# A hybrid attention layer on one core: the first pair's weight sums through small tiles, and the order in which the pairs of gate tiles begin

## The chip, the cores and the metric

The kernel runs on one core of one Trainium2 chip. The metric is device time in microseconds for one execution; lower is better. The time given for a version is the median of its runs.

## The reference

One decoder layer over 2048 tokens of width 1024 (plus 16 meta tokens in front). The rows of x are normed, multiplied by one wide matrix `w_in`, and the 6400 columns of the product go to two attentions and to gates:

```
xn = rms_norm(h, norm_gain)
proj = xn @ w_in                       # 1024 x 6400
sb_q, sb_k, sb_v, sw_q, sw_k, sw_v, sb_z, sw_z, g_sb, g_sw = split(proj)
o_sb = stick_breaking_attention(sb_q, sb_k, sb_v)
o_sw = sliding_window_sink_attention(rope(sw_q), rope(sw_k), sw_v, sinks)
y_sb = (o_sb * silu(sb_z)) @ w_branch_sb
y_sw = (o_sw * silu(sw_z)) @ w_branch_swa
merged = sigmoid(g_sb) * y_sb + sigmoid(g_sw) * y_sw
out = rms_norm(h + merged @ w_out, final_norm_gain)
```

The change concerns the columns `sb_z`, `sw_z`, `g_sb` and `g_sw`, the "gates": 28 column tiles of 128 columns each.

## The kernel before

**Numbers in two parts.** Every float32 operand of a matmul is split into a high part (a cast copy, on ScalarE) and a low part (the operand less the high part, on VectorE), and a product is three matmuls: high by high, high by low, low by high. A column tile of `w_in` is 128 x 1024; as weights it is 8 blocks of 128 x 128, high and low.

**The order of the work.** The tokens are worked in two halves of two groups of 512 (`halves`, line 1145). In each half come the projections with the sliding-window attention, then the stick-breaking attention, woven with gate tiles so that TensorE is fed, then the remaining gate tiles as "pairs". The branch and output projections (`finish`) stand at the end. TensorE's order is written out by hand (`manual_schedule`). The orders of ScalarE, VectorE and SyncE, which issues all DMAs, come from a planner: it runs through the program in an estimate of time, takes what is ready, earlier program text first, and gives tiles their buffers as these come free. Each engine's queue then runs strictly in that order.

**Gate tiles.** `gate` (line 580 on) asks for the tile's weights, multiplies them with the two groups (`gemm`, lines 415 to 417: 24 matmuls of 512 columns a group), takes a sigmoid on ScalarE (line 583) and stores the result. `weights` (line 167) loads a raw tile (512 KB), splits it (lines 109 and 112), and stores both parts to DRAM so that the second half can load them instead (`kept`). The weight buffers are a ring `wh`/`wl` of three tiles, the raw buffers a ring `raw` of two. `tmp` (line 344) is a ring of seven tiles of 128 x 512 that nearly all the helpers share.

**Pairs.** From gate tile 14 (counted from 0) on in half 0 (`REST[0] + 2`) and 20 in half 1, two column tiles are computed together by seven products of half-depth blocks in place of eight (the method of Strassen and Winograd). A pair's operands are sums of quarters. On the side of x they are made once a half by `sums_of_x` (lines 589 to 629): t1 to t4, some 50 VectorE instructions, in two steps. On the side of the weights `pair_weights` (line 631) makes t1 (the tile a as it is: quarters "11" and "12"), t3 (sums "s2" and "s3"), t2 ("s1" and "22", a plain quarter), and t4 ("s4"). t1, t3 and t2 each take one of the three `wh`/`wl` buffers. Pairs whose plain quarters half 1 wants as ordinary tiles (`plain`) also store those; the others store the sums for half 1 (`kept[key]`, in DRAM as p0 to p3).

`seven` (line 682) is a pair's matmuls in three parts: 11 (with 12, if `lead`), the middle (s2, 12 if not `lead`, s1, s3, 22), then s4. A product is 12 matmuls (line 688). The sum with product 11 at line 703 must be done before s3 may go on in the same PSUM bank. `in_line` (line 739) sets the order: the first pair's weights, the second step of the sums of x, pair one's 11 and 12, its middle, pair two's weights and 11, pair one's s4, and so on. Only the first pair of a half is `lead`.

**The early weights.** The first pair's weight sums of half 0 are made much earlier, at the start of the stick-breaking stage, between the second and third gate tile (lines 1354 to 1358): `pair_weights(..., early=True)` fills all three `wh`/`wl` buffers and five `tmp` tiles, stores the sums and the plain quarters (14 stores), and lets the buffers go. When the pairs begin, the sums are loaded again. The third gate tile's `weights` follows it in the program.

Of the kernel before, what the change touches and what calls it, by code (L numbers as in the profile page):

```python
# [17 lines left out]
P = 128  # L18
# [29 lines left out]
def tile_kernel(ctx, tc, x, xt, meta, metat, gain, w_in, w_sb, w_sw, w_out, sinks, fgain,  # L48
# [579 lines left out]
            parted("t4", k, b21)  # L628
        yield q

    def pair_weights(bp, ca, cb, plain, early=False):

        t1, t3, t2 = ([wp.tile([P, KT, P], F32R, tag=t, name=t, bufs=3) for t in ("wh", "wl")] for _ in range(3))
        if early:
            t4 = [tmp(F32R).rearrange("p (k c) -> p k c", k=KT // 2) for _ in range(2)]
        else:
            t4 = [bp.tile([P, KT // 2, P], F32R, tag=t, name=t, bufs=2) for t in ("s4h", "s4l")]
        key = w_in.name, ca, cb
        if key in kept:
            for ts, ks in zip((t1, t3, t2, t4), kept[key]):  # L640
                for t, k in zip(ts, ks):
                    DMA(t, k)
        else:
            a, b = load(ca), load(cb)
            s = tp.tile([P, KT, P], F32, tag="vt", name="s", bufs=1)
            s4 = tmp().rearrange("p (k c) -> p k c", k=KT // 2)
            lo, hi = slice(0, KT // 2), slice(KT // 2, KT)

            def parts(hl, t):
                A.copy(hl[0], t)  # L650
                V.tensor_tensor(hl[1], t, f32(hl[0]), op=ALU.subtract)
            parts(t1, a)
            if plain:
                t5 = [tmp(F32R).rearrange("p (k c) -> p k c", k=KT // 2) for _ in range(2)]
                parts(t5, b[:, lo])
            V.tensor_tensor(s[:, hi], a[:, lo], b[:, lo], op=ALU.subtract)
            V.tensor_tensor(b[:, lo], b[:, lo], b[:, hi], op=ALU.add)
            V.tensor_tensor(s[:, lo], b[:, lo], a[:, lo], op=ALU.subtract)
            parts(t3, s)
            parts(t2, b)  # L660
            V.tensor_tensor(s4, a[:, hi], s[:, lo], op=ALU.subtract)
            parts(t4, s4)
            if plain:
                for c in (ca, cb):
                    kept[w_in.name, c] = [dram(f"{e}_{w_in.name}_{c}", [P, KT, P], F32R) for e in "hl"]
                for k, t in zip(kept[w_in.name, ca], t1):
                    DMA(k, t)
                for k, t, u in zip(kept[w_in.name, cb], t5, t2):
                    DMA(k[:, lo], t)
                    DMA(k[:, hi], u[:, hi])  # L670
            if early or not plain:
                kept[key] = []
                for n, ts in enumerate((t1, t3, t2, t4)):
                    kept[key].append([dram(f"p{n}{e}_{ca}", list(t.shape), F32R) for e, t in zip("hl", ts)])
                    for k, t in zip(kept[key][n], ts):
                        DMA(k, t)
        (t1h, t1l), (t3h, t3l), (t2h, t2l) = t1, t3, t2
        lo, hi = slice(0, KT // 2), slice(KT // 2, KT)
        return {"11": (t1h[:, lo], t1l[:, lo]), "12": (t1h[:, hi], t1l[:, hi]), "s2": (t3h[:, lo], t3l[:, lo]),
                "s3": (t3h[:, hi], t3l[:, hi]), "s1": (t2h[:, lo], t2l[:, lo]), "22": (t2h[:, hi], t2l[:, hi]), "s4": t4}  # L680

    def seven(w, b, tag, use, lead):

# [37 lines left out]
    def gate_pair(bp, ga, gb, groups, q, tag, plain, lead, times):  # L721
        tiles = ga, gb

        def use(m, n, t):
            c0, dst, silu, src = tiles[m]
            e = tmp()
            A.activation(e, t, AF.Sigmoid)
            if silu:
                V.tensor_tensor(e, t, e, op=ALU.mult)
            if times:  # L730
                o = ring_x()
                DMA(o, src[groups[n]])
                V.tensor_tensor(e, e, o, op=ALU.mult)
            DMA(dst[groups[n]], e)
        w = pair_weights(bp, ga[0], gb[0], plain)
        yield
        yield from seven(w, q, tag, use, lead)

    def in_line(pairs):

        for n, g in enumerate(pairs):
            if n == 0:
                next(g)
                yield n
                next(g)
            next(g)
            if n + 1 < len(pairs):
                next(pairs[n + 1])
                next(pairs[n + 1])
            drain(g)  # L750
            yield n

# [553 lines left out]
    for half, groups in enumerate(halves):  # L1306
# [42 lines left out]
        with tc.tile_pool(name=f"sb{half}", bufs=1, side="left") as bp:  # L1349
            hsplit[0] = vsplit[0] = True  # L1350
            next_sums = {g: sums() for g in halves[1]} if half == 0 else {}
            side = stick(groups, bp, [(x[g * GT + i * P:g * GT + (i + 1) * P, f * GT:(f + 1) * GT], ssq[:, f, i:i + 1])
                                      for g, ssq in next_sums.items() for i in range(4) for f in range(2)])
            drain(tiles_by_tile(gts[1:2], groups))
            rest = REST[half]
            if half == 0:
                pair_weights(None, gss[0][rest + 2][0], gss[0][rest + 3][0], True, True)
            drain(tiles_by_tile(gts[2:3], groups))
            cost_sb = 8 * sum(4 * (4 - g) for g in groups) * 1.31 + 8 * 0.75
            ratio = cost_sb / ((rest - 3) * 10.4)  # L1360
            weave(tiles_by_tile(gts[3:rest], groups), side, ratio)
            drain(side)
        with tc.tile_pool(name=f"pairs{half}", bufs=1, side="left") as bp:
            ts = [mk() for mk in gts[rest:rest + 2]]
            sums_q = sums_of_x(bp, groups)
            tq = next(sums_q)
            for n, (w, use, _) in enumerate(ts):
                for i, g in enumerate(groups):
                    drain(lagged(col_tile(w, g, use, bank="gz"[i])))
            order = gss[half]  # L1370
            todo = in_line([gate_pair(bp, order[n], order[n + 1], groups, tq, ("o", "zm")[n // 2 % 2],
                                      half == 0 and n < PLAIN, n == rest + 2, half == 0) for n in range(rest + 2, 26, 2)])
            next(todo)
            next(sums_q)
            for n in todo:
                if half == 0 and n == 4:
                    t, u = (tmp()[:, :8] for _ in range(2))
                    for n, ssq in enumerate(next_sums.values()):
                        V.tensor_tensor(t[:, 4 * n:4 * n + 4], ssq[:, 0], ssq[:, 1], op=ALU.add)
                    rs = tp.tile([P, 8], F32, tag="rs8", name="rs", bufs=1)  # L1380
                    rsqrt(rs, t, tp, t=u)
                    rs0, rs1 = rs[:, :4], rs[:, 4:]
# [71 lines left out]
```

## Time and profile before

| | |
|---|---|
| median of 3 runs | 2140.8 us (2137.91 to 2143.49) |
| the profiled execution | 2139.68 us |
| its span, first to last instruction | 2138.0 us |
| mean granted TensorE clock | 0.995 |
| DMA queue of the kernel | 395.26 MB, 54.5% of 16 engines' span |

The profile shows one execution. PE is TensorE's matmuls, PEld its weight loads, DVE VectorE, ACT ScalarE, POOL GpSimd, SP SyncE; "SPq" is a DMA's time in SyncE's queue. A line of a view in order of time gives the start, the duration, the engine, the source line, the operation, the tile written and the tiles read, and in brackets the idle time before it and what ended it. "L109" is line 109 of the kernel. In the view of stages the columns are the length, then each engine's busy time, the granted clock, the DMA share and GB/s.

The 40 slices of the page, of 53.5 us each, show where TensorE is not full: the first slice and the last, and the eighth and thirteenth with an 8, the former with the clock at 9 tenths.

```profile
PE   8999999899998999999999999999999999999998
PEclk9999999899999999999999999999999999999999
```

### The profile page before, as it was taken

To read this page: it belongs to the slowest core of one execution; us is meant where nothing else is said; L and a number is where in the kernel's file an instruction comes from. 1 tells how busy PE (TensorE), PEld (TensorE's weight loads), DVE (VectorE), ACT (ScalarE), POOL (GpSimd) and SP (SyncE) were. 2 spreads that over 40 slices of the span, in tenths; PEclk is the share of its full clock that TensorE was granted. 3 is DMA by queue.
4 is the path that set the end of the run, shared out by engine and by line. 5 is a ranking of instruction groups with operands and counts; after the bars stand their busy time and mean duration, and the time that the engine had idled before them with its cause. 6 is when DMAs were issued, how large, how long until landed. Compare 5 with 4: busy or idle time off the path is not lost.

```text
span 2138.0 us, 29936 instructions
## 1 busy us (share of the span) xinstructions
PE 2091.8 (98%) x10426; PEld 1736.9 (81%) x10426; DVE 1497.1 (70%) x2389; ACT 1079.3 (50%) x2442; POOL 184.1 (9%) x373
## 2 busy tenths in 40 slices
PE   8999999899998999999999999999999999999998
PEld 7788887678877888888888888888888888887887
DVE  7897885578887863777756888989996336554453
ACT  6677774566643343677754656656552312221121
POOL 2122331000000000122210000000000000000000
PEclk9999999899999999999999999999999999999999
DMA  9855544975446985444446333333226786558532
GB/s 340 301 169 191 180 166 171 348 226 176 151 147 214 339 306 177 152 147 146 154 159 186 116 107 119 124 119 108 81 89 217 263 322 197 191 204 284 156 111 79
DMA packets 181142, 397.16 MB, mean 186 GB/s; under 512 B 23456, under 2 KB 41696, under 8 KB 180992
## 3 DMA queue, kind: packets, MB, share of 16 engines
q1 hardware_dynamic: 180992, 395.26, 54.5%
q8 instruction: 82, 1.34, 0.3%
q14 instruction: 68, 0.56, 0.1%
HBM read 245.74 MB, written 149.37 MB: 185 GB/s over the span
## 4 chain that ended last, share of the span: by engine, by line
PE 82%; DVE 8%; DMA 5%; ACT 3%; issue 2%; SPq 1%; DVEq 0%; ACTq 0%
PE ps_g L415 11%; PE ps_g L417 11%; PE ps_g L416 11%; PE ps_o L1106 5%; PE ps_t L1075 5%; PE ps_z L1050 5%; PE ps_o L934 3%; PE ps_z L888 2%; PE ps_z L688 2%; PE ps_t L688 2%; PE ps_g L688 2%; PE ps_g L237 1%; PE ps_g L238 1%; PE ps_g L236 1%; PE ps_z L238 1%
## 5 line engine op out<-in xcount | busy, mean ns | idle before, releaser
L415 PE MATMUL ps_g<-xh,wh 128*128 128x512 f32 x1224 | 503.2, 411 | 19.1 <-ACT wh L109 12.3
L416 PE MATMUL ps_g<-xl,wh 128*128 128x512 f32 x1224 | 481.4, 393 | 0.0
L417 PE MATMUL ps_g<-xh,wl 128*128 128x512 f32 x1224 | 481.2, 393 | 0.0
L415 PEld LDWEIGHTS ps_g<-xh,wh 128*128 128x128 f32 x1224 | 231.8, 189 | 56.1 <-ACT wh L109 12.7
L417 PEld LDWEIGHTS ps_g<-xh,wl 128*128 128x128 f32 x1224 | 230.7, 188 | 52.6 <-DVE wl L112 0.8
L416 PEld LDWEIGHTS ps_g<-xl,wh 128*128 128x128 f32 x1224 | 232.2, 190 | 36.0 <-DVE xl L1159 1.3
L1053 ACT ACTIVATE row<-ps_z 128x512 f32<-128x512 f32 (+2 forms) x320 | 165.4, 518 | 180.0 <-PE ps_z L1050 176.5
L1062 DVE TENSOR_TENSOR_SCAN row<-row 128x528 f32<-128x528 f32 (+1 forms) x192 | 210.6, 1097 | 19.8 <-ACT row L1053 15.4
L116 DVE SCALAR_TENSOR_TENSOR wtl<-ps_t,wth 128x512 fp32r<-128x512 f32 (+1 forms) x320 | 189.7, 593 | 18.5 <-ACT wth L115 17.8
L115 ACT ACTIVATE wth<-ps_t 128x512 fp32r<-128x512 f32 (+1 forms) x320 | 170.6, 533 | 58.3 <-PE ps_t L1075 56.0
L1060 DVE TENSOR_TENSOR_SCAN row<-row,mask 128x512 f32<-128x512 f32 (+4 forms) x128 | 144.2, 1131 | 69.1 <-ACT row L1053 68.0
L1050 PE MATMUL ps_z<-kt,q 128*128 128x512 f32 (+4 forms) x640 | 178.9, 355 | 0.0
L1075 PE MATMUL ps_t<-ident,row 128*128 128x128 f32 x1088 | 171.9, 273 | 6.3 <-DVE wtl L116 3.8
L1075 PEld LDWEIGHTS ps_t<-ident,row 128*128 128x128 f32 x1088 | 134.4, 140 | 41.1 <-DVE wtl L116 6.7
L1050 PEld LDWEIGHTS ps_z<-kt,q 128*128 128x128 f32 x640 | 117.4, 188 | 22.1 <-ACT row L1053 0.4
L1106 PE MATMUL ps_o<-wth,vc 128*128 128x512 f32 (+1 forms) x320 | 130.7, 409 | 1.0 <-ACT tmp L1110 0.9
L896 ACT ACTIVATE sc<-sc,nm 128x129 f32<-128x129 f32 x256 | 100.0, 393 | 40.9 <-DVE nm L894 40.2
L1106 PE MATMUL ps_o<-wtl,vc 128*128 128x512 f32 (+1 forms) x320 | 117.1, 366 | 0.2
L112 DVE TENSOR_TENSOR wl<-raw,wh 128x1024 fp32r<-128x1024 f32 (+1 forms) x51 | 58.4, 1145 | 45.6 <-ACT wh L109 40.8
L1066 POOL COPY xs<-row 128x16 f32<-128x16 f32 x128 | 28.8, 225 | 668.8 <-DVE row L1062 590.1
L583 ACT ACTIVATE tmp<-ps_g 128x512 f32<-128x512 f32 x72 | 43.1, 598 | 65.2 <-PE ps_g L417 60.2
L301 ACT ACTIVATE sq<-res 128x512 bf16<-128x512 f32 x32 | 20.2, 632 | 109.3 <-DVE res L297 107.0
(421 smaller groups left out, 4132.5 us busy)
## 6 DMA issues: line engine op xcount, KB each, us to landing
wh<-h_in_w_in SPq DMA_DIRECT2D x60, 512.0 KB
wl<-l_in_w_in SPq DMA_DIRECT2D x60, 512.0 KB
raw<-in_w_in SPq DMA_DIRECT2D x50, 512.0 KB
h_in_w_in<-wh SPq DMA_DIRECT2D x41, 512.0 KB
l_in_w_in<-wl SPq DMA_DIRECT2D x41, 512.0 KB
q<-qd SPq DMA_DIRECT2D x128, 128.0 KB
vc<-vd SPq DMA_DIRECT2D x48, 256.0 KB
kd<-tmp SPq DMA_DIRECT2D x32, 256.0 KB
```

The costliest lines, as they stand in the source:

```text
L115: A.activation(h, acc, AF.Copy, scale=scale)
L116: V.scalar_tensor_tensor(l, acc, scale, f32(h), op0=ALU.mult, op1=ALU.subtract)
L415: T.matmul(acc, lhsT=wh[:, k, :], rhs=xh[g][:, k, :], start=k == 0, stop=False)
L416: T.matmul(acc, lhsT=wh[:, k, :], rhs=xl[g][:, k, :], start=False, stop=False)
L417: T.matmul(acc, lhsT=wl[:, k, :], rhs=xh[g][:, k, :], start=False, stop=k == KT - 1)
L688: T.matmul(acc, lhsT=l[:, k, :], rhs=r[:, k, :], start=first and k == i == 0, stop=k == KT // 2 - 1 and i == 2, skip_group_check=not (firs ...
L1050: T.matmul(acc[:, :b - a], lhsT=lq, rhs=kt[h][:, k0 + a:k0 + b], start=t == 0, stop=t == 1)
L1053: A.activation(r[:, a:b], acc[:, :b - a], AF.Sigmoid, scale=-1.0)
L1060: V.tensor_tensor_scan(r[:, :w], r[:, :w], mask[0][:, :w], 1.0, op0=ALU.mult, op1=ALU.max)
L1062: V.tensor_tensor_scan(r[:, :w], r[:, :w], r[:, :w], last[j], op0=ALU.mult, op1=ALU.min)
L1075: T.transpose(tr[:, j * P:(j + 1) * P], rows_of[h, g, n - (j > i), j][:, k0:k0 + P], ident)
L1106: T.matmul(o[:, :n], lhsT=v, rhs=r, start=first and r is wh, stop=last and r is wl)
```

## The change

Three things are edited.

1. `pair_weights(..., early=True)` becomes a function of its own, `early_weights`. It makes the same sums, but a quarter (128 x 512) at a time, each in two `tmp` tiles, and stores each quarter to where it belongs, a plain one that is also a kept tile's to both places: 22 stores of 256 KB. It takes no `wh`/`wl` buffer. It works in place on the raw tiles: the last sum is taken from the first tile's raw buffer.
2. At the start of the stick-breaking stage the second and third gate tiles' weights are both asked for before the early weights, and their matmuls come after it. TensorE's order there stays as it was.
3. `pair_weights` gives t1 first and the rest later; the first two pairs of each half are `lead` instead of the first; and `in_line` begins with 11 and 12 of pair one, 11 and 12 of pair two, and then pair one's middle. Of a later pair t1 and product 11 still stand ahead of the s4 of the pair before, and the rest of its weights is asked for after that.

```diff
+    def early_weights(ca, cb):
+        key = w_in.name, ca, cb
+        kept[key] = [[dram(f"p{n}{e}_{ca}", [P, 4 if n == 3 else KT, P], F32R) for e in "hl"] for n in range(4)]
+        for c in (ca, cb):
+            kept[w_in.name, c] = [dram(f"{e}_{w_in.name}_{c}", [P, KT, P], F32R) for e in "hl"]
+        plain_a, plain_b = (kept[w_in.name, c] for c in (ca, cb))
+        t1, t3, t2, t4 = kept[key]
+        a, b = load(ca), load(cb)
+        lo, hi = slice(0, KT // 2), slice(KT // 2, KT)
+        def part(t, *dst):
+            for e in range(2):
+                u = tmp(F32R).rearrange("p (k c) -> p k c", k=KT // 2)
+                if e == 0:
+                    h = u
+                    A.copy(u, t)
+                else:
+                    V.tensor_tensor(u, t, f32(h), op=ALU.subtract)
+                for d, cs in dst:
+                    DMA(d[e][:, cs], u)
+        s = tp.tile([P, KT, P], F32, tag="vt", name="s", bufs=1)
+        part(a[:, lo], (t1, lo), (plain_a, lo))
+        part(a[:, hi], (t1, hi), (plain_a, hi))
+        part(b[:, lo], (plain_b, lo))
+        part(b[:, hi], (t2, hi), (plain_b, hi))
+        V.tensor_tensor(s[:, hi], a[:, lo], b[:, lo], op=ALU.subtract)
+        part(s[:, hi], (t3, hi))
+        V.tensor_tensor(b[:, lo], b[:, lo], b[:, hi], op=ALU.add)
+        part(b[:, lo], (t2, lo))
+        V.tensor_tensor(s[:, lo], b[:, lo], a[:, lo], op=ALU.subtract)
+        part(s[:, lo], (t3, lo))
+        V.tensor_tensor(a[:, hi], a[:, hi], s[:, lo], op=ALU.subtract)
+        part(a[:, hi], (t4, lo))
...
+    def pair_weights(bp, ca, cb, plain):
...
+        t1 = ring("11", "12")
+        key = w_in.name, ca, cb
+        old = kept.get(key)
+        if old:
+            fill(t1, old[0])
         else:
             a, b = load(ca), load(cb)
+            A.copy(t1[0], a)
+            V.tensor_tensor(t1[1], a, f32(t1[0]), op=ALU.subtract)
+        yield w
+        t3, t2 = ring("s2", "s3"), ring("s1", "22")
+        t4 = w["s4"] = [bp.tile([P, KT // 2, P], F32R, tag=t, name=t, bufs=2) for t in ("s4h", "s4l")]
+        if old:
+            for ts, ks in zip((t3, t2, t4), old[1:]):
+                fill(ts, ks)
...
-        w = pair_weights(bp, ga[0], gb[0], plain)
+        ws = pair_weights(bp, ga[0], gb[0], plain)
+        w = next(ws)
         yield
-        yield from seven(w, q, tag, use, lead)
+        products = seven(w, q, tag, use, lead)
+        next(products)
+        yield
+        next(ws)
+        yield
+        yield from products
 
     def in_line(pairs):
 
+        first, second = pairs[:2]
+        next(first)
+        yield 0
+        for step in (first, first, second, second):
+            next(step)
         for n, g in enumerate(pairs):
-            if n == 0:
-                next(g)
-                yield n
+            if n:
                 next(g)
             next(g)
-            if n + 1 < len(pairs):
-                next(pairs[n + 1])
-                next(pairs[n + 1])
+            for more in pairs[n + 1:n + 2] if n else ():
+                next(more)
+                next(more)
             drain(g)
             yield n
...
-            drain(tiles_by_tile(gts[1:2], groups))
             rest = REST[half]
+            ts = [mk() for mk in gts[1:3]]
             if half == 0:
-                pair_weights(None, gss[0][rest + 2][0], gss[0][rest + 3][0], True, True)
-            drain(tiles_by_tile(gts[2:3], groups))
+                early_weights(gss[0][rest + 2][0], gss[0][rest + 3][0])
+            for t in ts:
+                drain(by_group([t], groups))
...
-                                      half == 0 and n < PLAIN, n == rest + 2, half == 0) for n in range(rest + 2, 26, 2)])
+                                      half == 0 and n < PLAIN, n < rest + 6, half == 0) for n in range(rest + 2, 26, 2)])
```

More of the change, by code (lines that the diff above doesn't have):

```diff
@@ L629, in sums_of_x @@
         yield q
[L631 to L637, printed above, removed]
-        key = w_in.name, ca, cb
[L639 to L642, printed above, removed]
+    def early_weights(ca, cb):
+        key = w_in.name, ca, cb
+        kept[key] = [[dram(f"p{n}{e}_{ca}", [P, 4 if n == 3 else KT, P], F32R) for e in "hl"] for n in range(4)]
[28 more added lines that the diff above has]
+        part(a[:, hi], (t4, lo))
@@ new lines, in pair_weights, with ring, fill @@
+    def pair_weights(bp, ca, cb, plain):
+        lo, hi = slice(0, KT // 2), slice(KT // 2, KT)
+        w = {}
+        def ring(n, n2):
+            t = [wp.tile([P, KT, P], F32R, tag=t, name=t, bufs=3) for t in ("wh", "wl")]
+            w[n], w[n2] = ([u[:, c] for u in t] for c in (lo, hi))
+            return t
+        def fill(ts, ks):
+            for t, k in zip(ts, ks):
+                DMA(t, k)
+        t1 = ring("11", "12")
[3 more added lines that the diff above has]
+            fill(t1, old[0])
@@ L643, in pair_weights @@
         else:
             a, b = load(ca), load(cb)
+            A.copy(t1[0], a)
[6 more added lines that the diff above has]
+                fill(ts, ks)
+        else:
             s = tp.tile([P, KT, P], F32, tag="vt", name="s", bufs=1)
@@ L646, in pair_weights @@
             s4 = tmp().rearrange("p (k c) -> p k c", k=KT // 2)
-            lo, hi = slice(0, KT // 2), slice(KT // 2, KT)
             def parts(hl, t):
@@ L651, in parts @@
                 V.tensor_tensor(hl[1], t, f32(hl[0]), op=ALU.subtract)
-            parts(t1, a)
             if plain:
@@ L670, in pair_weights @@
                     DMA(k[:, hi], u[:, hi])
-            if early or not plain:
+            if not plain:
                 kept[key] = []
@@ L676, in pair_weights @@
                         DMA(k, t)
[L677 to L680, printed above, removed]
+        yield w
     def seven(w, b, tag, use, lead):
```

## The prediction, made before the changed kernel was run

> **What bounds the kernel now.** I read the page first, then who waited for whom on TensorE, then the order in time of each engine's instructions around the three places that the change touches, and last the chain that ended last.
>
> ```profile
> span 2138.0 us, 29936 instructions
> PE 2091.8 (98%) x10426; PEld 1736.9 (81%) x10426; DVE 1497.1 (70%) x2389; ACT 1079.3 (50%) x2442; POOL 184.1 (9%) x373
> ```
>
> TensorE is busy for all but 46 us of the span. The change leaves out no matmul, so it can gain only from those 46 us and from stretches in which matmuls run slowly after a pause.
>
> ```profile
> PE ps_g L415 <- ACT wh L109: 12.3, 1, 12.3
> ...
> PE ps_z L688 <- DVE tmp L703: 4.6, 2, 3.5
> ```
>
> The largest wait is one of 12.3 us, at the third gate tile of half 0, the one that is computed just after the early weights. The waits on L703 are those of the first pair in each half. Both are in the change's reach. The early place in time, on ScalarE:
>
> ```profile
> 341.55 1.05 ACT L650 CAST wh<-raw 128x1024 fp32r<-128x1024 f32 x1 [0.57 <-PE ps_g L416]
> ...
> 366.12 0.60 ACT L583 ACTIVATE tmp<-ps_g 128x512 f32<-128x512 f32 x1 [4.88 <-PE ps_g L417]
> 371.56 0.60 ACT L583 ACTIVATE tmp<-ps_g 128x512 f32<-128x512 f32 x1 [4.84 <-PE ps_g L417]
> 372.06 0.61 ACT L650 CAST tmp<-raw 128x512 fp32r<-128x512 f32 x1
> 382.70 1.04 ACT L109 CAST wh<-raw 128x1024 fp32r<-128x1024 f32 x1 [5.31 <-DMA raw<-in_w_in]
> ```
>
> The two sigmoids close the two groups of the second gate tile, 5.44 us apart: that is what 24 matmuls cost at full rate. Only behind the second one does ScalarE begin on the pair's second weight tile (372.06), and only then can the raw buffers come free. SyncE shows the rest:
>
> ```profile
> 328.27 0.42 SPq L58 DMA_DIRECT2D raw<-in_w_in  x1
> 351.82 8.81 SPq L58 DMA_DIRECT2D gs<-tmp  x2
> 365.77 1.17 SPq L58 DMA_DIRECT2D kt<-kd  x2
> 376.77 0.55 SPq L58 DMA_DIRECT2D raw<-in_w_in  x1
> ```
>
> The third gate tile's raw weights are asked for at 376.77 and are in use at 382.70, 5.9 us later. TensorE has had nothing since 371.5.
>
> ```profile
> 392.70 0.60 ACT L583 ACTIVATE tmp<-ps_g 128x512 f32<-128x512 f32 x1 [8.96 <-PE ps_g L417]
> ```
>
> The next group closes at 392.70, 21.14 us after the one before instead of 5.44. So this place loses 15.7 us: the wait of 12.3 and 3.4 of matmuls at a lower rate after it.
>
> **Part 1, the early weights through small tiles.** The second and third gate tiles now ask for their weights before the early work does, and the early work uses no large weight buffers. So the third tile's raw load takes the place of the one at 328.27, and its split the place that L650 has at 341.55 (that cast waited for TensorE to release a weight buffer, as this split will).
>
> ```profile
> 343.69 1.20 DVE L651 TENSOR_TENSOR wl<-raw,wh 128x1024 fp32r<-128x1024 f32 x1
> 372.70 0.69 DVE L651 TENSOR_TENSOR tmp<-raw,tmp 128x512 fp32r<-128x512 f32 x1 [10.58 <-ACT tmp L650]
> ```
>
> With VectorE's half at 343.69 the third tile is ready at 344.9, 26 us before it is wanted. The 15.7 us go.
>
> What is late next is the fourth tile, wanted 2 x 5.44 us after 371.56, at 382.4. Its raw buffer is one of the two that the early work holds. That work moves: the first tile's load to 328.3, the second's to 344.9, when the third tile's split frees a buffer. It is eight parts, each a cast of 0.6 us (372.06), a subtraction of 0.69 (372.70) and 2 or 4 stores of 256 KB, and four sums of 0.69: 4.8 us of ScalarE and 8.3 of VectorE, against 4.3 and 7.8 before. SyncE issues 22 stores instead of 14, for the same 5.5 MB. Six parts, 12 tiles, hang on the second load. It lands at about 349.7 (344.9 and the 4.79 us of a quiet 512 KB load, row below); 12 tiles through 7 buffers are two rounds, each about 1.3 us of compute and 5.5 of a store (a 256 KB load of x took 5.46, row below), so an estimate for the last is 363.3. Then 5.9 us for the fourth tile's load and 2.3 for its split give 371.5, 11 us ahead. The cover is this stretch:
>
> ```profile
> 345.00:355.00 10.00, 8.89 (x41) 6.55 (x41) 5.71 (x12) 5.90 (x14) 2.68 (x5) 1.00 0.75 292
> 355.00:365.00 10.00, 10.00 (x47) 8.13 (x46) 2.36 (x5) 2.37 (x4) 1.54 (x3) 1.00 0.22 80
> ```
>
> From 355 to 365 VectorE and ScalarE work 2.4 us of 10, and DMA moves 80 GB/s. Ahead of that the attention's last units are still on both engines, in order: between 345 and 355 TensorE loses 1.11 us beside the large cast and subtraction that stand there today. More short instructions in those queues could cost that once more, or nothing; I charge 1.1. Bounds: 0 to 4.
>
> **Part 2, the pairs of half 0.** TensorE's new order is 11 and 12 of pair one, 11 and 12 of pair two, then pair one's middle.
>
> ```profile
> 396.28 5.46 DMA xq<-in_x
> 415.74 9.09 DMA raw<-in_w_in
> 590.06 4.79 DMA raw<-in_w_in
> 652.16 4.61 PE ps_z L688 x12
> 669.40 2.72 PE ps_g L688 x12
> 1624.27 3.04 PE ps_z L688 x12
> ```
>
> A product of 12 matmuls costs 2.72 us, 4.61 after a pause of 3.5 us and 3.04 after one of 1.06 us (the rows of both pauses follow).
>
> ```profile
> 643.04 0.39 PE L688 MATMUL ps_z<-t2h,wh 128*128 128x512 f32 x1
> 652.16 0.50 PE L688 MATMUL ps_z<-t3h,wh 128*128 128x512 f32 x1 [3.52 <-DVE tmp L703]
> 665.42 0.50 PE L688 MATMUL ps_z<-t2h,wh 128*128 128x512 f32 x1 [0.50 <-ACT wh L650]
> 666.83 0.50 PE L688 MATMUL ps_z<-t2h,wl 128*128 128x512 f32 x1 [0.68 <-DVE wl L651]
> ```
>
> Lost today: 3.52 at L703 (VectorE is still at the sums of x), 1.9 of slow matmuls after it, 0.5 and 0.68 at pair two: 6.6 us. Two products, 5.44 us, now stand ahead of pair one's middle, and pair two has both its plain products behind it and its buffer free early, so I take all 6.6 as gone. But pair two's plain products need pair two's first weights, and there are three large buffers: pair one's first, second and third tiles are asked for ahead of them.
>
> ```profile
> 643.02 1.06 ACT L650 CAST wh<-raw 128x1024 fp32r<-128x1024 f32 x1 [1.91 <-PE ps_zm L688]
> ```
>
> ```profile
> 646.08 1.22 DVE L651 TENSOR_TENSOR wl<-raw,wh 128x1024 fp32r<-128x1024 f32 x1
> ```
>
> Today pair two's cast waits until pair one's product 12 (ps_zm) has ended and so freed the buffer, and the subtraction ends at 647.30, behind the sums of x in VectorE's queue. Today TensorE does other products meanwhile; now product 11 of pair two is next, and all of TensorE's queue, pair one's middle first, is behind it. From 643.04 to 647.30 only its first two matmuls (0.45 us) can run: 3.8 us idle. Bounds: 2.0, if VectorE subtracts straight behind the cast, to 5.5. It falls into a piece of 1.1 us and one of 2.7, between the two pauses priced above (0.3 and 1.9); I charge 0.5 for slow matmuls, nearer the short one. So -6.6 and +4.3: -2.3 us.
>
> The Trainium skill (TensorE: Matmul & The Clock Gate, Part 1) has the matmul rate halve after a whole idle window of about 3.4 us and come back after as long a time of work. By that rule neither piece would cost anything here and the sum would be 0.5 lower; the row at 652.16 agrees, that at 1624.27 lost 0.3 without such a window.
>
> **Part 3, the pairs of half 1.** Here the weights are loaded as kept.
>
> ```profile
> 1585.37 0.32 SPq L58 DMA_DIRECT2D wh<-p0h  x1
> 1601.25 0.32 SPq L58 DMA_DIRECT2D wh<-p1h  x1
> 1612.13 0.32 SPq L58 DMA_DIRECT2D wh<-p2h  x1
> 1617.57 0.32 SPq L58 DMA_DIRECT2D wh<-p0h  x1
> 1617.99 0.38 SPq L58 DMA_DIRECT2D wl<-p0l  x1
> ```
>
> ```profile
> L688 PE MATMUL ps_z<-t2h,wh x8: 389/389/389, 1617.6 to 1637.3; 128*128 128x512 f32 x8
> ```
>
> ```profile
> 1624.27 0.50 PE L688 MATMUL ps_z<-t3h,wh 128*128 128x512 f32 x1 [1.06 <-DVE tmp L703]
> ```
>
> The three large buffers go to p0, p1 and p2 of the first pair; the second pair's p0 is asked for at 1617.57, the moment at which product 12 of the first has ended (1617.6) and its buffer is free. In the new order product 11 of the second pair is due at that moment. Its second half is issued at 1617.99; with 4.79 us for a quiet load it is usable at 1622.8, so TensorE idles 5.2 less 0.45 us, 4.7, and pays 1.9 for the slow matmuls: +6.6. What goes is 1.06 and 0.3. Net +5.2 us. Bounds: 3 (a landing 2 us sooner) to 9.5 (9.09 us in a loaded queue).
>
> Nothing else moves in cost: later pairs ask for their second and third weights after the pair before has ended, but those buffers were freed by that pair's middle before too, 8.2 us (three products) ahead of need.
>
> **The sum.** The profiled execution took 2139.7 us. -15.7 + 1.1 - 2.3 + 5.2 = -11.7, so 2128.0; the runs' median, 2140.8, is 1.1 above that execution, so **2129**. Own range of this case: 2124 to 2136, from the bounds of each part.
>
> **The rivals.**
>
> *The pair waits go too.* If the planner gives the second pair's first weights a buffer before the first pair's third tile, the four products run on. For it: the third tile is only needed five products, 13.6 us, after the pairs begin. Against it: buffers went in program order in both halves (rows of 1585 to 1618). Time: 2139.7 - 15.7 + 1.1 - 6.6 - 1.4 = 2117, as a median **2118**. Chance 0.16.
>
> *The stall moves to the fourth tile, in part.* If the early work's last cast is planned behind a gate sigmoid, as the one at 372.06 was, the raw buffer is late. Behind the sigmoid of 377.0: load until 383.4, split until 385.7, 3.3 us and 1.9 of slow matmuls; behind that of 382.4 about 5.4 more. Between them, 7.5: **2137**. For it: the planner did so before, with seven small tiles. Against it: the gate tiles' own work is now emitted after the early work. Chance 0.18.
>
> *Slower: the small stores hold the small tiles.* 16 tiles must pass through 7 buffers that gates and attention use as well. If those leave five and each store takes as long as a transfer in the loaded stretch (9.09 us), four rounds of 9.5 us from 351 end at 389; load and split (11.4 us) give 400.5, 18 us after the fourth tile is wanted, and 3.4 of slow matmuls: 21.4 for the 15.7 removed. With the other terms 2149.4, as a median **2150**. It decides from the point at which the last early store lands later than about 380. SyncE's 8.81 us on one gate store (351.82) show how a queue can hold stores up; the quiet 355 to 365 speaks against it. Chance 0.08.
>
> The Trainium skill (DMA: Bandwidth & Descriptors, Bandwidth) asks for transfers of 1 MiB or more, and so speaks against this change, which cuts 512 KB stores into 256 KB ones. No run here shows yet whether that matters.
>
> **How the numbers follow.** Forecast 0.46, the three rivals 0.16, 0.18 and 0.08, and 0.12 for a replanned order that shifts small waits elsewhere (3 to 5 us either way about the forecast or about no change). The range takes the first three: 2116 to 2142. This kernel's measurement tells 0.3%, 6.4 us, from no change: 2134.4 and 2147.2. Faster: 0.44 of the forecast, 0.16, 0.04 of the second rival, 0.04: 0.68. Slower: 0.06 of the third rival and 0.03: 0.09. The rest, 0.23, is no change.
>
> **What would show it.** Right: no wait of over 3 us on L109 by TensorE; casts of the early parts before 370; after product 12 of the first pair an idle of about 4 us on a weight buffer in half 0 and about 5 on a load in half 1, in place of L703. Wrong: a wait of the fourth gate tile on its raw load (second and third rival), or four products without a pause in half 1 (first rival).

## The result, and the profile after

The changed kernel takes **2159.36 us** (median of 4 runs, 2158.13 to 2164.21) where the kernel before took 2142.14 on the same chip: a ratio of 1.0087, 95% interval 1.0064 to 1.0110. It is slower by 0.9%. The forecast was 2129, faster; the range ended at 2142 and did not hold it.

The profiled execution took 2158.13 us. First the page, with the span and the busy time of each engine:

```profile
span 2156.4 us, 29957 instructions
PE 2098.1 (97%) x10426; PEld 1740.6 (81%) x10426; DVE 1500.1 (70%) x2394; ACT 1080.8 (50%) x2445; POOL 181.8 (8%) x373
```

TensorE is busy 6.3 us more with the same 10426 matmuls, so some ran slowly, and idle 12.1 us more (58.3 in place of 46.2). Who waited for whom on TensorE (total, times, longest):

```profile
PE ps_z L733 <- ACT wh L699: 11.7, 2, 5.9
PE ps_t L1129 <- DVE wtl L116: 7.6, 7, 2.5
...
PE ps_g L415 <- ACT tmp L583: 5.4, 1, 5.4
PE ps_z L1104 <- DMA q<-qd: 3.8, 2, 3.6
PE ps_g L733 <- DMA wh<-p0h: 3.3, 1, 3.3
PE ps_g L733 <- DVE wl L687: 2.5, 1, 2.5
...
PE ps_g L733 <- ACT wh L686: 0.9, 1, 0.9
```

The 12.3 us on L109 are gone, and so are the 4.6 on the sum that was line 703. The last three rows are the new wait of Part 2 (0.9 and 2.5) and that of Part 3 (3.3). Not in the forecast is the first row: two pauses of 5.9 us in the pairs, on a cast of L699, the split of t3 (s2 and s3). The attention's waits on q, and longer ones of its transposes on VectorE, were not in it either.

The time by stage, from the starts of the first and last product matmul (L688 before, L733 after):

| us | before | after | difference | forecast |
|---|---|---|---|---|
| start of the pairs, half 0 | 637.6 | 639.5 | +1.9 | -14.6 |
| pairs, half 0 | 122.9 | 136.2 | +13.3 | -2.3 |
| pairs, half 1 | 58.2 | 62.1 | +3.9 | +5.2 |
| the rest | | | -0.7 | 0 |
| span | 2138.0 | 2156.4 | +18.4 | -11.7 |

So two of three parts failed: the gain in front of the pairs didn't arrive, and the pairs of half 0 lost what nobody had counted.

**The early place.** ScalarE, in order of time:

```profile
342.42 1.05 ACT L109 CAST wh<-raw 128x1024 fp32r<-128x1024 f32 x1 [0.55 <-PE ps_g L416]
...
360.98 1.66 ACT L647 CAST tmp<-raw 128x512 fp32r<-128x512 f32 x3
...
374.55 0.62 ACT L647 CAST tmp<-raw 128x512 fp32r<-128x512 f32 x1 [2.13 <-DMA l_in_w_in<-tmp]
376.10 0.60 ACT L583 ACTIVATE tmp<-ps_g 128x512 f32<-128x512 f32 x1 [0.93 <-DMA p1l<-tmp]
...
384.02 0.60 ACT L583 ACTIVATE tmp<-ps_g 128x512 f32<-128x512 f32 x1 [0.38 <-PE ps_g L417]
```

The third gate tile's split is there at 342.42, as forecast, and its first group closes at 384.02, 8.7 us before the 392.70 of the kernel before. But the eight early parts (L647) run from 360.98 to 375, not from 350 to 363, and from the fourth on most wait for a store to give a small tile back. The second gate tile's sigmoid (376.10) stands behind the last of them in ScalarE's queue: that is TensorE's 5.4 us on L583. SyncE's queue:

```profile
351.67 8.79 SPq L58 DMA_DIRECT2D gs<-tmp  x2
...
361.62 0.32 SPq L58 DMA_DIRECT2D p0h<-tmp  x1
...
376.58 0.43 SPq L58 DMA_DIRECT2D raw<-in_w_in  x1
...
380.57 0.53 SPq L58 DMA_DIRECT2D p3l<-tmp  x1
```

All 22 early stores go out between 361.6 and 381.1. What that stretch is like, by stages of 15 us (length, busy time of PE, PEld, DVE, ACT, POOL, then the granted clock, the DMA share and GB/s), before:

```profile
360.00:375.00 15.00, 11.52 (x51) 9.12 (x49) 3.04 (x6) 2.70 (x6) 0.90 (x3) 1.00 0.60 183
375.00:390.00 15.00, 6.17 (x14) 4.39 (x15) 4.75 (x5) 3.43 (x4) 0.00 (x0) 0.54 0.98 354
390.00:405.00 15.00, 15.00 (x71) 12.29 (x70) 5.67 (x7) 7.97 (x19) 2.07 (x4) 1.00 1.04 350
...
420.00:435.00 15.00, 14.78 (x79) 11.66 (x78) 10.54 (x14) 9.69 (x22) 0.79 (x4) 1.00 0.90 272
```

And after:

```profile
360.00:375.00 15.00, 11.34 (x50) 9.07 (x49) 7.58 (x12) 5.20 (x10) 0.85 (x2) 1.00 0.91 333
375.00:390.00 15.00, 13.26 (x52) 10.82 (x53) 1.92 (x2) 3.56 (x6) 0.00 (x0) 0.89 0.96 293
390.00:405.00 15.00, 10.43 (x50) 7.62 (x48) 7.43 (x9) 7.29 (x18) 1.83 (x4) 1.00 0.97 320
...
420.00:435.00 15.00, 11.41 (x54) 9.15 (x54) 6.28 (x9) 6.87 (x19) 1.51 (x3) 0.89 0.92 286
```

Read the column of the DMA share first: it is 0.90 or more from 375 to 435 in both kernels, wherever TensorE's pause lies. Before, TensorE lost 3.5 us between 360 and 375, 8.8 between 375 and 390, and then ran full up to 435. (This is the eighth slice of the page of before; its clock digit there is 8, not 9.) After, it loses 3.7 and 1.7 in the first two, 4.6 between 390 and 405, and 3.6 between 420 and 435. By the sums of the same view over 345 to 450, TensorE is busy 87.99 us before and 87.15 after: the wait that was removed came back in pieces.

**The pairs of half 0.** ScalarE, before the first of the two new pauses:

```profile
670.49 0.63 ACT L772 ACTIVATE tmp<-tmp 128x512 f32<-128x512 f32 x1 [2.09 <-DVE tmp L763]
671.02 0.60 ACT L699 CAST tmp<-raw 128x512 fp32r<-128x512 f32 x1
674.45 1.04 ACT L699 CAST wh<-s 128x1024 fp32r<-128x1024 f32 x1 [2.82 <-issue]
```

The cast into tmp at 671.02 is t5, pair two's plain quarter, and takes two small tiles. It comes only behind the last sigmoid of pair one's sums (L772). VectorE's subtraction and the sums for s follow, then t3's cast at 674.45. TensorE stands from before that:

```profile
675.55 0.79 PE L733 MATMUL ps_z<-t2h,wh 128*128 128x512 f32 x1 [5.87 <-ACT wh L699]
```

In the chain that ended last, the matmuls behind the two pauses:

```profile
676.81 4.18 PE ps_z L733 x10
...
701.70 3.71 PE ps_z L733 x10
```

Ten matmuls take 2.27 us at full rate (2.72 for 12), so the pauses cost 1.9 and 1.4 more. The two waits, 11.7, and these 3.3 make 15.0 us. With the new wait ahead of them (0.9 and 2.5, and 1.9 of slow matmuls) and without the 6.6 that went, that is 13.7 for the 13.3 of the table.

### The profile page after: what moved, and what is told of

It reads as the page before. It is cut to its first block, busy times and chain, and to the rows that moved or that the text cites. A ratio compares the mean times of both kernels' runs of the same rounds, so it can differ in the third digit from the quotient of the medians.

```text
span 2156.4 us, 29957 instructions
## 1 busy us (share of the span) xinstructions
PE 2098.1 (97%) x10426; PEld 1740.6 (81%) x10426; DVE 1500.1 (70%) x2394; ACT 1080.8 (50%) x2445; POOL 181.8 (8%) x373
## 4 chain that ended last, share of the span: by engine, by line
PE 85%; DVE 5%; DMA 4%; ACT 3%; issue 1%; SPq 1%; ACTq 0%; DVEq 0%
PE ps_g L415 11%; PE ps_g L416 11%; PE ps_g L417 11%; PE ps_o L1160 5%; PE ps_t L1129 5%; PE ps_z L1104 5%; PE ps_z L942 3%; PE ps_o L988 3%; PE ps_z L733 2%; PE ps_t L733 2%; PE ps_g L733 2%; PE ps_g L237 1%; PE ps_g L238 1%; PE ps_g L236 1%; PE ps_z L237 1%; PE ps_z L238 1%
## 5 line engine op out<-in xcount | busy, mean ns | idle before, releaser
L942 PEld LDWEIGHTS ps_z<-kk,q 128*128 128x128 f32 x512 | 69.7, 190 | 6.6 <-DVE q L923 0.7
```

Source lines behind the costliest of these rows:

```text
L942: T.matmul(acc[:, a * 256:(a + 1) * 256], lhsT=lq, rhs=kk[:, 2 * kv + hl, blk * P:(blk + 2) * P], start=hl == 0, stop=hl == 1)
```

## The experiments

The first question was whether the loss is the pairs' alone and whether the early part gains anything by itself; the theories stand in each expectation. The ratio of each run is to the kernel before, timed beside it on the same chip.

**One part at a time.** The first kernel takes only the new early weights, with the pairs in the order of before; the second takes only the pairs' new order.

```diff
 # e1_early_only: the kernel before, with
-            drain(tiles_by_tile(gts[1:2], groups))
+            ts = [mk() for mk in gts[1:3]]
...
+                early_weights(gss[0][rest + 2][0], gss[0][rest + 3][0])
 # e2_pairs_only: the changed kernel, with the early weights of before
```

> Only the early weights through small tiles and the two gate tiles asked for ahead of them; the pairs as before. Theory A (the profile after: the third gate tile's wait shrinks from 12.3 to 5.4 us, but the stores now end as late as before and the first rows wait for loads of x and q, so the 9 us gained by 390 us are gone by 440): within 3 us of before, 2139 to 2145 us. Rival B (the early part is itself a large part of the loss): 2147 us or more. Rival C (the early part gains and the pairs cost all): 2134 us or less.

Measured: 2141.48 us, 1.0002 (0.9990 to 1.0014).

> Only the pairs' new order; the early weights as before. Theory A (the pairs of half 0 take 136.6 instead of 123.3 us, those of half 1 62.4 instead of 58.7): 17 us slower than before, 2157 to 2161 us. Rival B: half of that or less, up to 2150 us.

Measured: 2160.31 us, 1.0094 (1.0075 to 1.0112). Its pairs of half 0 take 138.1 us, and the wait of 12.6 at the third gate tile is back. So the whole loss is the pairs', and the early part is worth nothing, in either company.

**What holds the pairs up.** Two candidates: the place in the program at which the rest of the next pair's weights is asked for, now behind the s4 of the pair before; or the small tiles that t5 takes, which the pair before holds through its middle.

```diff
 # e3_rest_ahead: in_line, ahead of s4
-            if n:
-                next(g)
             next(g)
-            for more in pairs[n + 1:n + 2] if n else ():
-                next(more)
+            for more in pairs[n + 1:n + 2]:
+                if n:
+                    next(more)
+                    next(more)
                 next(more)
             drain(g)
 # e4_own_t5: t5 in the buffers of s4, not in tmp
-                t5 = [tmp(F32R).rearrange("p (k c) -> p k c", k=KT // 2) for _ in range(2)]
+                t5 = [bp.tile([P, KT // 2, P], F32R, tag=t, name=t, bufs=2) for t in ("s4h", "s4l")]
...
```

> The changed kernel, but the rest of the next pair's weights is asked for ahead of the s4 product again, as before; the four plain products still begin. Theory A (the two waits of 5.9 and 5.8 us on the cast of t3 come from the place in the program: the plain quarter's two small tiles are given out behind the sigmoid that follows s4): those two waits shrink to about 1 us each and the slow matmuls behind them go, so 11 to 15 us below the changed kernel, 2144 to 2148 us. Rival B (the waits come from the three weight buffers, or from the second pair's weights standing ahead of the first pair's middle): unchanged, 2157 to 2161 us.

Measured: 2154.34 us, 1.0066 (1.0051 to 1.0082); half 0 takes 131.8. TensorE's pauses of this kernel are shorter, not gone:

```profile
674.46 0.79 PE L733 MATMUL ps_z<-t2h,wh 128*128 128x512 f32 x1 [3.75 <-ACT wh L699]
697.25 0.50 PE L733 MATMUL ps_z<-t2h,wh 128*128 128x512 f32 x1 [2.46 <-ACT wh L699]
```

> The changed kernel, but the plain quarter of a pair's second tile takes buffers of the s4 tag in place of two of the seven small tiles; the place in the program is the changed kernel's. Theory A1 (the seven small tiles are what holds it): the two waits shrink as in the run before, 2144 to 2149 us. Theory A2 (the place in the program alone sets the order on ScalarE and VectorE, whichever buffer it takes): unchanged, 2157 to 2161 us.

Measured: 2143.00 us, 1.0008 (0.9997 to 1.0018). In its ScalarE queue t3's cast stands some 20 us earlier:

```profile
653.20 1.05 ACT L700 CAST wh<-s 128x1024 fp32r<-128x1024 f32 x1 [1.91 <-PE ps_o L735]
```

Both pauses of 5.9 us are gone, and half 0 takes 119.4 us: 3.5 less than before, where 2.3 less was forecast. With the program's order untouched, the two small tiles of t5 make 0.8%, about 17 us (1.0087 less 1.0008). Asking earlier makes 0.2% of it (1.0087 less 1.0066).

**Half 1.** The same kernel, with the order of before in half 1 alone.

```diff
 # e8_own_t5_half0
-    def in_line(pairs):
+    def in_line(pairs, both):
-        for step in (first, first, second, second):
+        for step in (first, first, second, second)[:4 if both else 2]:
...
-            half == 0 and n < PLAIN, n < rest + 6, half == 0) for n in range(rest + 2, 26, 2)])
+            half == 0 and n < PLAIN, n < rest + (6 if half == 0 else 4), half == 0) for n in range(rest + 2, 26, 2)], half == 0)
```

> The changed kernel with the plain quarter in buffers of its own, and in half 1 the order of before (only the first pair is ahead with its plain products). Theory A (in half 1 the second pair's first weights can only be loaded when the first pair's product 12 has freed a buffer, so the new order costs 4.7 us there): pairs of half 1 take 58 us again instead of 62.9, 2137 to 2140 us. Rival B (half 1 loses for another reason, as the sums of x): 61 us or more there, 2142 to 2145 us.

Measured: 2138.21 us, 0.9993 (0.9983 to 1.0002); half 1 takes 58.3 us in place of 62.9. The loss of half 1 is that of the reload, as forecast. In the changed kernel SyncE and TensorE show it:

```profile
1632.80 0.32 SPq L58 DMA_DIRECT2D wh<-p0h  x1
```

```profile
1636.29 0.76 PE L733 MATMUL ps_g<-xh,wh 128*128 128x512 f32 x1 [3.29 <-DMA wh<-p0h]
```

**Where the early gain goes: not to the loads of x.** ScalarE waits 11.6 us for loads of x between 385 and 450 in the kernel with the early part alone, 4.0 between 390 and 460 before. So these loads were put three steps later, with the new early part and, as a control, without it.

```diff
 # e5_early_x_later (on e1), e6_before_x_later (on the kernel before)
-                if n1 > 1:
-                    for src, acc in squared[2 * n1 - 4:2 * n1 - 2]:
+                if n1 > 4:
+                    for src, acc in squared[2 * n1 - 10:2 * n1 - 8]:
```

> The early weights alone (pairs as before), and the loads of x whose squares the second half needs begin three head-and-group steps later in the stick-breaking stage. Theory A (the 8 us that the small tiles gain by the third gate tile are lost because ScalarE waits in order for loads of x behind the 22 stores, 11.6 us in 8 waits): the gain is kept in good part, 2131 to 2136 us. Rival B (the stage is limited further on by VectorE's scans or by the loads of q and k): 2139 to 2143 us, as the early part alone.

> The kernel before with the same later loads of x, as a control. Theory A: before, ScalarE waits only 4.0 us for x in that stretch and TensorE is 13 us behind anyway: 2137 to 2142 us, so that the gain of the run above is not the shift's alone. Rival B (the shift itself is what gains): as low as the run above.

Measured: 2140.90 us, 0.9998 (0.9989 to 1.0008), and 2141.41, 0.9999 (0.9989 to 1.0008). Nothing in either; this theory fell.

**When the early parts run.** They were to start at the tile's arrival. One kernel asks for them ahead of the last attention units in the program; another also gives the first tile's two parts tiles of their own (the tables of the rotary embedding, unused by then).

```diff
 # e7_early_ahead (on e1): behind the weave of the window's last units
+            if m:
+                ts2 = [mk() for mk in gts[1:3]]
+                early_weights(gss[0][rest + 2][0], gss[0][rest + 3][0])
...
 # e9_own_early (on e7)
-                u = tmp(F32R).rearrange("p (k c) -> p k c", k=KT // 2)
+                u = own.pop() if own else tmp(F32R)
...
```

> The early weights alone, asked for in the program ahead of the last attention units instead of behind them. Theory A (the planner holds the eight parts back until 361 us because the small tiles go to what stands earlier in the program): the first store goes out by 352 us instead of 362, the fourth gate tile and the first rows come sooner, 2131 to 2138 us. Rival B (the attention's last units wait for small tiles or stand behind the parts in ScalarE's and VectorE's queues): 2140 us or more. Rival C (the stores stay behind the gate store in SyncE's queue until 360 us): 2139 to 2143 us.

Measured: 2141.03 us, 1.0001 (0.9991 to 1.0011). The first casts come at 359.28: the place in the program doesn't move them.

> The early weights alone, ahead of the last attention units in the program, with the first tile's two parts in four tiles of the sliding-window stage that are free by then (the cosine and sine tables) and the other six parts in the shared small tiles. Theory A (the parts start only at 361 us because no shared small tile is given out before; from there to 430 us the DMA queue is full, and TensorE's wait only moves from place to place): the first part's casts run by 345 us, up to 2 MB of stores go out before 361, and the stretch to the end of the full queue gets shorter by 2 to 6 us: 2135 to 2139 us. Rival B (SyncE's wait of 8.8 us at the gate store, from 351 to 360 us, holds the stores back whatever tile they come from): the casts run early, the stores do not, 2139 to 2143 us.

Measured: 2137.57 us, 0.9979 (0.9970 to 0.9988). The parts with tiles of their own are made and stored some 25 us earlier, on ScalarE and SyncE:

```profile
334.85 0.62 ACT L650 CAST sn<-raw 128x512 fp32r<-128x512 f32 x1
```

```profile
335.50 0.33 SPq L58 DMA_DIRECT2D p0h<-sn  x1
...
343.03 1.14 SPq L58 DMA_DIRECT2D l_in_w_in<-ct  x1
```

So it is the small tiles that hold the parts back until 361. Eight stores (2 MB) less in the loaded stretch are worth 0.2% here, but this kernel has a new loss of its own, at the first row of the attention:

```profile
390.76 0.55 PE L1091 MATMUL ps_z<-kt,q 128*128 128x256 f32 x1 [6.64 <-DMA gs<-tmp]
```

The attention's first load (kt) goes out at 381.05, where e1 has it at 374.14: asked for earlier in the program, the early part's loads and stores now stand ahead of it in SyncE's queue (gs<-tmp in the row is only the DMA that came last). e7 has the same wait (6.82 us, first load at 384.88). So 0.2% is not the full price of those stores.

**How many bytes.** The rest of the gain could lie in the bytes. Four of the eight parts store plain quarters for half 1, 2 MB in all. They are left out here, together with the one part made only for that; half 1 then loads those two tiles raw and splits them again. It was done to the early part alone (e10) and to the kernel before (e14).

```diff
 # e10_no_plain_stores (on e1)
...
-        part(a[:, lo], (t1, lo), (plain_a, lo))
-        part(a[:, hi], (t1, hi), (plain_a, hi))
-        part(b[:, lo], (plain_b, lo))
-        part(b[:, hi], (t2, hi), (plain_b, hi))
+        part(a[:, lo], (t1, lo))
+        part(a[:, hi], (t1, hi))
+        part(b[:, hi], (t2, hi))
 # e14_before_no_plain (on the kernel before), in two places
-            if plain:
+            if plain and not early:
```

> The early weights alone, without the eight stores of plain quarters (2 MB of 5.5) and without the part that only they need; the second half splits these two tiles from raw weights instead. Theory A (between 361 and 430 us the stage goes at the pace of the DMA queue, 320 to 340 GB/s): 2 MB less are 6 us less there, 2133 to 2138 us. Rival B (the stage waits for the order of ScalarE's and VectorE's work, not for bytes): 2139 to 2143 us.

Measured: 2126.50 us, 0.9929 (0.9914 to 0.9944). The gain lies ahead of the pairs: those of half 0 begin at 623.8 us in place of 637.6, and from their end to the end of the kernel it takes 1378.3 us, before 1377.5. So half 1, which splits two tiles more, neither gains nor loses. The stages 375 to 390 and 420 to 435 of this kernel:

```profile
375.00:390.00 15.00, 13.52 (x63) 10.86 (x61) 4.33 (x5) 4.01 (x8) 1.82 (x4) 1.00 1.01 330
...
420.00:435.00 15.00, 14.16 (x78) 11.47 (x77) 12.36 (x16) 12.50 (x31) 0.59 (x3) 1.00 0.94 328
```

> The kernel before, early weights in the large buffers, but without the stores of plain quarters. Theory A (fewer bytes help only a stage that the DMA queue bounds; here the third gate tile waits for a raw buffer first): its wait of 12.3 us stays within 3 us, 2135 to 2141 us, so the small tiles are needed for the gain. Rival B (the fewer stores alone gain): 2126 to 2130 us.

Measured: 2131.17 us, 0.9963 (0.9949 to 0.9977). The wait at the third gate tile is gone here too, with the early part in the large buffers: half of the 0.71% (0.37) comes without the change. ScalarE shows why:

```profile
350.33 1.04 ACT L650 CAST wh<-s 128x1024 fp32r<-128x1024 f32 x1
354.10 1.05 ACT L650 CAST wh<-raw 128x1024 fp32r<-128x1024 f32 x1 [0.20 <-DMA p1h<-wh]
...
363.05 1.05 ACT L109 CAST wh<-raw 128x1024 fp32r<-128x1024 f32 x1 [0.35 <-DMA raw<-in_w_in]
...
374.47 0.61 ACT L650 CAST tmp<-tmp 128x512 fp32r<-128x512 f32 x1
```

In the kernel before, these two casts come at 374.88 and 375.83, behind the cast into a small tile at 372.06 (t5, the plain quarter). Without t5 they run more than 20 us earlier, the raw buffer comes free, and the third tile's split is there at 363.05; only the last cast, which still takes small tiles, is late. So by these rows the first wait of 12.3 us, too, stood behind two small tiles, as the pauses in the pairs do; that it was only they isn't tried alone. This run takes out t5 and 2 MB of stores at once and lets other stores go out earlier (p1 and p2 from 351 to 359), so it doesn't tell what the bytes are worth.

**The same bytes put back.** To tell bytes from the other things that e10 leaves out, 2 MB of plain stores of another tile, which hold no small tile and which nobody reads, were added to e10. The first try put them where the planner liked; the second pins them behind the last early part.

```diff
 # e13_extra_stores (on e10)
+        for i in range(4):
+            DMA(dram(f"extra{i}", [P, KT, P]), s)
         part(s[:, lo], (t3, lo))
 # e15_extra_late (on e10)
         part(a[:, hi], (t4, lo))
+        V.tensor_copy(s[:, :, 0:1], f32(mx[:, :, 0:1]))
+        for i in range(4):
+            DMA(dram(f"extra{i}", [P, KT, P]), s)
```

> The early weights without the plain stores, as in the run before, plus four stores of 512 KB (2 MB) of the tile of differences to DRAM that nothing reads, at the same place and holding no small tile. Theory A (the bytes in the full DMA queue cost the time): back to 2136 to 2142 us. Rival B (what cost the time was that a small tile is held for two stores and that there were eight parts instead of seven, with the sigmoid of the second gate tile behind them): about 2127 us, at most 2130. Between them: both.

Measured: 2129.75 us, 0.9949 (0.9935 to 0.9962). But they went out at 353.45, into the quiet stretch, which then had 289 GB/s (e10 without them: 164):

```profile
353.45 2.85 SPq L58 DMA_DIRECT2D extra<-s  x4
```

```profile
345.00:365.00 20.00, 19.84 (x91) 15.57 (x90) 12.79 (x25) 10.45 (x22) 3.91 (x6) 1.00 0.79 289
```

So it wasn't the test that was meant; it shows that there 2 MB cost little, 0.2% with overlapping intervals, and TensorE is full beside them. It also has the same 14 stores (3.5 MB) left for the loaded stretch as e9, and is 0.30% faster than e9: the bytes in that stretch are not all that counts; the place of the attention's loads in SyncE's queue is the likely rest (first kt at 368.06 here, 381.05 in e9).

> As the kernel without plain stores, plus four stores of 512 KB of the tile of differences that nothing reads, now tied by a small write behind the last reader of that tile, so that they fall at about 370 us into the full DMA queue and still hold no small tile. Theory A (bytes in the full queue cost the time): 2132 us or more, towards 2140. Theory D (the second tile's plain first quarter costs it: it must have two small tiles before the sums may overwrite it, so all sums and six parts stand behind it): 2126 to 2130 us.

Measured: 2140.49 us, 0.9995 (0.9986 to 1.0004). Now they go out behind 371, one and then three:

```profile
371.69 0.38 SPq L58 DMA_DIRECT2D extra<-s  x1
373.61 3.13 SPq L58 DMA_DIRECT2D extra<-s  x3
```

The same stages as of e10 above, and the largest wait of TensorE between 340 and 470:

```profile
375.00:390.00 15.00, 8.59 (x37) 6.64 (x35) 1.22 (x1) 2.25 (x3) 0.00 (x0) 0.83 1.04 389
...
420.00:435.00 15.00, 11.56 (x51) 8.99 (x50) 8.34 (x12) 7.58 (x18) 0.59 (x3) 0.89 0.85 257
```

```profile
PE ps_z L1084 <- DMA q<-qd: 9.5, 3, 5.4
```

The whole gain of e10, 0.66% or 14 us, is gone with 2 MB in four stores that hold no small tile and stand ahead of most of the attention's loads. TensorE waits for the attention's q, whose first load goes out at 381.29 in place of 377.97.

**Which bytes.** What was left open is whether it is the number of bytes or the one part made for half 1 alone, which stands ahead of all the sums.

```diff
 # e16_plain_b_only (on e10): that part and its 0.5 MB back
+        part(b[:, lo], ([dram(f"b{e}", [P, KT, P], F32R) for e in "hl"], lo))
 # e17_all_but_plain_b (on e1): all but that part, 1.5 MB
-        part(b[:, lo], (plain_b, lo))
```

> As the kernel without plain stores, but the second tile's first quarter is split and stored plain as in the changed kernel (to a place that nothing reads): 8 parts and 16 stores, 0.5 MB more. Theory D: most of the 14 us come back, 2135 to 2141 us. Theory A: 0.5 MB are 1.5 us, 2126 to 2130 us.

> As the changed early part alone, without only the split and the store of the second tile's plain first quarter: 7 parts, 20 stores, 1.5 MB of plain stores stay (the second half splits the second tile from raw weights). Theory D: the gain stays, 2126 to 2131 us. Theory A: three quarters of the bytes are back, 2135 to 2139 us. Theory E (six tiles are held for two stores each): 2133 us or more as well; A and E are then told apart by the run with late extra stores.

Measured: 2129.13 us, 0.9941 (0.9929 to 0.9954), and 2140.24, 0.9994 (0.9986 to 1.0003). The 0.5 MB cost 0.12% over e10 (the intervals overlap), the 1.5 MB 0.65%, all 2 MB (e1) 0.73%. So it isn't that one part, and the price grows with the bytes. But the waits lie elsewhere than in e15: between 340 and 470 TensorE waits 5.3 us on the gate's sigmoid (L583, behind the early casts) and 4.5 on q in e1, 4.0 and 2.9 in e17, none and 9.5 in e15. In e1 and e17 small tiles are also held for two stores each. The bytes alone are enough to take the gain (e15); that the held tiles have no share in e1 isn't shown.

**Both mended.** The early part of e10 with the pairs of e8.

> Both parts mended: the early weights through small tiles without the plain stores, the four plain products in half 0 only, with the plain quarter of a pair's second tile in buffers of the s4 tag. If the parts add (14.7 us from the one, 3.5 from the other): 2121 to 2125 us. Rival (the shared small tiles or another bound takes the second gain back): 2126 us or more.

Measured: 2123.39 us, 0.9922 (0.9909 to 0.9935): the lowest of all and ahead of both kernels, but not clear of e10. The gains of e10 (0.71%) and e8 (0.07%, itself not clear of nothing) have the sum that was measured; that they add isn't shown. In the profiled executions half 0's pairs take 119.7 us in place of e10's 122.9, and begin 1.5 later.

## Why the prediction was wrong

**Part 1, right in its first step and wrong in its sum.** The third gate tile's split came where it was forecast (342.42), the wait on L109 is gone, the tile closes 8.7 us earlier. The step that failed is "12 tiles through 7 buffers are two rounds ... the last is 363.3", with the quiet stretch 355 to 365 as its cover. The small tiles were not to be had before 361 (by the rows of e14 they had held the cast at 372.06 in the kernel before, too), and the parts ran after the cover, in the stretch in which the queue is full. There the removed wait had been hiding: TensorE paused from 375 to 390, but DMA ran at 354 GB/s meanwhile, and the attention that follows wants what was loaded then (q, kt and vc, its queries, keys and values). Taking TensorE's pause away without taking bytes away moved it to the sigmoids behind the early casts, to q and to the transposes; e15 shows that 2 MB of stores there are enough to take the whole gain of e10. I had counted "the same 5.5 MB" as no change, when the time at which they are stored mattered. The rule of the Trainium skill that I cited against the change (DMA: Bandwidth & Descriptors, Bandwidth: 1 MiB or more in a transfer) is not what decided: e9 keeps all 22 stores of 256 KB, only eight of them earlier, and is faster than the kernel before, and e10, with 14 stores of 256 KB, is faster than e14, which keeps the large ones.

**Part 2, the sentence "Nothing else moves in cost".** It counted the three large buffers and found them free 8.2 us ahead of need. The weights of a pair with plain quarters also need two of the seven small tiles, and in the new order the pair before, still in its middle with its product sums, holds small tiles at that time. That cost about 17 us, more than the whole forecast gain of 11.7. The code of the change shows it: t5 is taken from `tmp`, the ring of seven. The terms that I did count came near. The wait at L703 went. The new wait, forecast at 3.8 us in a piece of 1.1 and one of 2.7, came as 0.91 and 2.49 (on TensorE):

```profile
645.99 0.50 PE L733 MATMUL ps_g<-xh,wh 128*128 128x512 f32 x1 [0.91 <-ACT wh L686]
...
649.21 0.50 PE L733 MATMUL ps_g<-xh,wl 128*128 128x512 f32 x1 [2.49 <-DVE wl L687]
```

The slow matmuls behind it were mis-sized, 0.5 for 1.9. A window over them has the clock:

```profile
649.20:652.50 3.30, 3.29 (x9) 2.60 (x10) 3.30 (x6) 1.22 (x2) 0.00 (x0) 0.56 0.42 164
```

The chain has 4.14 us for ten matmuls from 649.21, 1.9 over the 2.27 of full rate. The Trainium skill (TensorE: Matmul & The Clock Gate, Part 1) has the rate halve after a whole idle window of about 3.4 us. The trace disagrees here: two matmuls stood between the idle pieces, the longest was 2.49 us, and the clock fell to 0.56 all the same. Here the two pieces, 3.40 us together, cost the same 1.9 us as the one pause of 3.52 in the kernel before, so they should have been priced as one.

**Part 3, right.** +3.9 for a forecast of +5.2. The idle time was 3.29 for 4.7, since the load was usable 3.5 us after its issue (1632.80 to 1636.29), not 4.8. The slow matmuls after it took the 1.9 that was charged.

**The rivals.** The one that ended slower, "the small stores hold the small tiles", named the right resource and the wrong place and price. Its point of decision was reached (the last early store went out at 380.57), but the early part came out at no change, not at +9; the loss was in the pairs, which it didn't look at. The other two didn't come: TensorE has no wait on the fourth tile's split, and the four products of half 1 have the pause of 3.29 us between them.

**What stays open.** Which of their users keep the small tiles until 361 was not isolated: e7 excludes the place in the program and e9 shows that other tiles free the parts. How the loss of the early gain divides between bytes, small tiles held for two stores and the order of SyncE's queue is open. That 2 MB cost 14 us, where at 350 GB/s they take 6.0, is put down to the waits and slow matmuls that follow one another in that stretch; this is argued from the stage rows, not tried.

## What to carry to other kernels

When steps are moved, count every ring that they draw on, the small shared one too, and ask who holds its tiles at the new time; a buffer that is free 8 us early is no cover if its neighbour isn't. Before a wait is booked as gain, look at the DMA share of the stretch it lies in: if the queue is full there, a pause of the engine may be only where the shortage shows, and then it is bytes that have to go or to move out of the way of the loads that come next. What can be made again cheaply later may better not be stored in such a stretch, as the two tiles of e10.

## What was unexpected of the hardware

The price of the same 2 MB of stores was 0.66% (14 us) in a stretch with the queue at 330 GB/s and about 0.2%, with overlapping intervals, in one at 164 GB/s, 18 us earlier (e15 and e13 against e10). And the granted clock fell to 0.56 after idle pieces of 0.91 and 2.49 us with two matmuls between them.
